# A hybrid encoder's odd layer: tiles placed ahead of the decay sums, low parts of the first group made on chip, state products in two banks

## The chip, the cores and the metric

The kernel runs on one core of one Trainium2 chip. The metric is the device time of one execution in microseconds, the median of several. A core has a TensorE (PE, matmuls), a VectorE (DVE), a ScalarE (ACT), a GpSimd (POOL) and a SyncE (SP, which here only issues DMAs). TensorE writes to PSUM, from which VectorE and ScalarE read.

## The reference

Two layers and a last RMSNorm, on x of 512 positions by 1024, all in fp32. The even layer (latent attention beside a Conformer convolution) is not touched. The odd layer projects the normed x by one matrix and splits the result: a gate z, the convolved x, B and C of a bidirectional Mamba-2 mixer (24 heads in four groups), its raw time steps, and a short gated convolution:

```python
dt_f = jax.nn.softplus(dt_f_raw + dt_bias_f)            # 512 x 24, the same backward
a_f = -jnp.exp(a_log_f)
dA = (dt * a).reshape(b, c, l, g, r)                    # chunks of 128 positions
a_cs = jnp.cumsum(jnp.moveaxis(dA, 2, -1), axis=-1)     # sums of the decays in a chunk
L = jnp.exp(jnp.where(tri, a_cs[..., :, None] - a_cs[..., None, :], -jnp.inf))
...
decay_states = jnp.exp(a_cs[..., -1:] - a_cs)
states = jnp.einsum("bclgn,bcgrl,bclgrp->bcgrpn", Bc, decay_states, X)
```

The state that enters a chunk is the decayed state of the chunk before plus that chunk's product, in both directions.

## The kernel before, in words

A product of fp32 matrices is made of three passes of a reduced type (fp32r): each operand is split into a high part and a low part, and high x high, high x low and low x high are summed. A *channel tile* is 128 output channels of the odd projection by all 512 positions: 24 matmuls of 128x512, 16 with the high part of the weights and 8 with the low part (`mm_cm`, L317).

`Weights._prepare` (L79) brings a tile's weights: a load on SP into `w_raw`, a cast on ScalarE to `w_hi` (L91), and the low part `w_lo`. For the even layer and the z tiles that is one subtraction on VectorE or GpSimd (L96). For the other odd tiles (`BY_DMA`) ScalarE writes the negated high part (L93 in the listing, `w_lo` holding the negated copy), and a DMA issued by GpSimd adds `w_raw` to it on its way (L94). The buffers form small rings; a tile's load waits until the raw buffer's earlier user has been read, and its cast until TensorE has read the earlier high part.

The odd layer's tiles come in a fixed list: z, then C0, B0, x0, x1, x2, zc3, C1, ... `fill(n)` (L791) emits the next n tiles, and turns of earlier tiles behind them. A z tile also yields the raw steps `dtr`. The decay steps follow: softplus by an exponential (L804, ScalarE) and a chain of small VectorE operations on 128x192 (L805 to L817), which ends in `d1`, the product of step and decay. For each direction, `d1` is transposed on TensorE (L823, through the helper at L273), summed along the positions by four scans (L829), written to memory (`acs`, L830), and its sums `cs` are transposed back (L832); from these follow `nacs`, the chunk totals (L836) and the factors `dec`, `ea` and `eA`.

`ssd_states` (L882) makes, for a group, six state products (three chunks, two directions) of 128x384 in PSUM (L891); for the first chunk ScalarE copies the product, for the later ones GpSimd scales the state before (L896) and VectorE adds the product to it (L897). `bank` names the PSUM banks: acc has 3, cv 1, sb 2 and tp 2. Transposes of later work also use them. After the states come the transposes of the group before's normed output (`xs`, scaled at L984).

The order on each engine is set by a scheduler that places the emitted instructions; the code's order and the buffers are what it starts from. In the listings, `kc` holds the identity matrix, `d_4891` (or `d_4834` after) is `d1`.

Of the kernel before, what the change touches and what calls it, by code (L numbers as in the profile page):

```python
# [66 lines left out]
BY_DMA = ("C", "B", "x", "zc", "h", "gc", "gb", "zd")  # L67
EARLY = ("qkv", "a", "g", "uq", "uv", "uk", "zb", "za")


class Weights:
# [7 lines left out]
    def _prepare(self):  # L79
        nc = self.tc.nc  # L80
        key, ap, kt, n = self.slabs[self.i]
        eng = nc.vector if key in EARLY or key in ("oe", "oo") and self.i % 2 else nc.gpsimd
        self.i += 1
        more = key in BY_DMA and self.i % 3 == 0
        raw = (self.more if more else self.pool).tile([P, D], F32, name="w_raw", tag="w_raw",
                                                      bufs=1 if more else self.raw_bufs)[:, :kt * n]
        nc.sync.dma_start(raw, ap)
        more = key in BY_DMA and self.i % 4 == 0
        hi, lo = ((self.more if more else self.pool).tile([P, D], F32R, name=nm, tag=nm, bufs=1 if more else self.bufs)
                  [:, :kt * n] for nm in ("w_hi", "w_lo"))  # L90
        nc.scalar.copy(hi, raw)  # L91
        if key in BY_DMA:
            nc.scalar.mul(lo, raw, -1.0)  # L93
            nc.gpsimd.dma_start(lo, raw, accum_op=ALU.add)  # L94
        else:
            eng.tensor_tensor(lo, raw, hi.bitcast(F32), op=ALU.subtract)  # L96
        v = lambda t: t.rearrange("p (k n) -> p k n", k=kt)
        self.ready.append((key, v(hi), v(lo)))
# [5 lines left out]
    def next(self, key):  # L104
        self.fetch(self.ahead + (3 if key in BY_DMA else 1))
        k, hi, lo = self.ready.pop(0)
        assert k == key, (k, key)
        return hi, lo
# [69 lines left out]
def trunk(ctx, tc, A, out, dbg=None):  # L178
    nc = tc.nc
# [28 lines left out]
    def bank(tag):  # L208
        return ps.tile([P, S], F32, name=tag, tag=tag, bufs=banks[tag])
# [59 lines left out]
    def transposed(blocks, tag="tp", rows=P):  # L269

        tp = bank(tag)
        for j, b in enumerate(blocks):
            T.transpose(tp[:rows, j * P:(j + 1) * P], b, ident)  # L273
        return tp[:rows, :]
# [42 lines left out]
    def mm_cm(key, xT, kk=KT):  # L317

        wh, wl = W.next(key)
        a = bank("acc")  # L320
        xh, xl = xT
        seq = [p for k in range(kk) for p in ((wh[:, k], xh[k]), (wh[:, k], xl[k]))]
        seq += [(wl[:, k], xh[k]) for k in range(kk)]
        for n, (l, r) in enumerate(seq):
            T.matmul(a, l, r, start=n == 0, stop=n == 3 * kk - 1)  # L325
        return a
# [105 lines left out]
    for nm, o, w in (("q_norm", 0, 384), ("kv_norm", 384, 256)):  # L432
# [10 lines left out]
        for k in range(w // P):  # L443
            tp = transposed([qkv[t][:, o + k * P:o + (k + 1) * P] for t in range(NT)])
# [55 lines left out]
    tp = transposed([kr[:, t] for t in range(NT)], "tp", 96)  # L500
# [99 lines left out]
    for p in range(8):  # L600
# [15 lines left out]
        z = mm_cm("zb", xT)  # L616
# [19 lines left out]
    for h in range(2):  # L636
        for t in range(NT):
            tp = transposed([u[h * 4 + j][:, t * P:(t + 1) * P] for j in range(4)], "tp")
# [58 lines left out]
    def bc(col, n, w):  # L697

        return col.rearrange("p (n o) -> p n o", o=1).broadcast_to([P, n, w])

    def over_t(row, n):

        return row.rearrange("p (o n) -> p o n", o=1).broadcast_to([P, NT, n])
# [3 lines left out]
    def one(shape, name, dt=F32):  # L707
        return pg.tile(shape, dt, name=name)

    def tmp(name, tag, bufs, shape=(P, S), dt=F32):  # L710
        return pg.tile(list(shape), dt, name=name, tag=tag, bufs=bufs)

    def prow(nm):
        return rc[:, RC[nm][0]:RC[nm][0] + RC[nm][1]]
# [76 lines left out]
    def fill(n):  # L791

        for _ in range(n):
            before = list(turns)
            turns.clear()
            channel_tile(*next(todo))
            for t in before:
                t()

    fill(2)  # L800

    d1, d2, d3, dt = (one([P, NT, NH], n) for n in ("d1", "d2", "d3", "dt"))
    V.scalar_tensor_tensor(d1, dtr, -1.0, dtr, op0=ALU.mult, op1=ALU.min)
# [11 lines left out]
    aexp = one([P, NH], "aexp")  # L815
    SC.activation(aexp, prow("a_log"), AF.Exp)
    V.scalar_tensor_tensor(d1, dt, -1.0, over_t(aexp, NH), op0=ALU.mult, op1=ALU.mult)  # L817

    nacs = one([P, NT, NH], "nacs")
    acs = dr.tile([2, SH, S], F32, name="acs")  # L820
    back = bank("tp")
    for d in range(2):
        tp = transposed([d1[:, t, d * SH:(d + 1) * SH] for t in range(NT)], "tp", SH)  # L823
        cs = tmp("cs", "c5", 4)[:SH]
        for c in range(NT):
            o, i, z = cs[:, c * P:(c + 1) * P], tp[:, c * P:(c + 1) * P], ident[:SH]
            if d:
                o, i = o[:, ::-1], i[:, ::-1]
            V.tensor_tensor_scan(o, i, z, 0.0, op0=ALU.add, op1=ALU.bypass)  # L829
        nc.sync.dma_start(acs[d], cs)  # L830
        for c in range(NT):
            T.transpose(back[:, c * NH + d * SH:c * NH + (d + 1) * SH], cs[:, c * P:(c + 1) * P], ident[:SH, :SH])  # L832
    V.tensor_scalar(nacs, back[:, :NT * NH].rearrange("p (t h) -> p t h", t=NT), -1.0, None, op0=ALU.mult)
# [18 lines left out]
    def gw(name, bufs):  # L852
        return tmp(name, name, bufs, (P, GW))
# [4 lines left out]
    def heads(g):  # L858
        return [slice(d * SH + g * HPG, d * SH + (g + 1) * HPG) for d in range(2)]

    def ssd_products(g):

        CT, BT = inp[g]["C"], inp[g]["B"]
        cb = bank("tp")
        for c in range(NT):
            cc = slice(c * P, (c + 1) * P)
            T.matmul(cb[:, cc], BT[:, cc], CT[:, cc], start=c == 0, stop=c == 3, skip_group_check=True)
        cbm = [tmp("cbm", "cbm", 4) for _ in range(2)]
        for d in range(2):
            V.tensor_tensor(c4(cbm[d]), c4(cb), masks[d], op=ALU.mult)  # L870
        return cbm, [weighted(g, 0, d) for d in range(2)]

    def chunk(n, d):
        return NT - 1 - n if d else n

    def weighted(g, n, d):

        w, c = gw("gt", 5), chunk(n, d)
        V.tensor_tensor(h3(w), h3(inp[g]["x"][:, c]), bc(dec[:, c, heads(g)[d]], HPG, HD), op=ALU.mult)
        return w  # L880

    def ssd_states(g, first):  # L882

        Bt = inp[g]["Bt"]
        St = [[None] * NT for _ in range(2)]
        for n in range(NT - 1):
            for d in range(2):
                c, nxt = chunk(n, d), chunk(n + 1, d)
                w = weighted(g, n, d) if n else first[d]
                sp = bank("tp")  # L890
                T.matmul(sp[:, :GW], Bt[:, c * P:(c + 1) * P], w, start=True, stop=True)  # L891
                st = St[d][nxt] = gw("St", 12)
                if n == 0:
                    SC.copy(st, sp[:, :GW])
                else:
                    G.tensor_tensor(h3(st), h3(St[d][c]), bc(eA[:, c, heads(g)[d]], HPG, HD), op=ALU.mult)  # L896
                    V.tensor_tensor(st, sp[:, :GW], st, op=ALU.add)  # L897
        return St
# [122 lines left out]
        op[1].append(lo)  # L1021


    fill(5)
    cbm, first = ssd_products(0)
    St = ssd_states(0, first)
    for g in range(GRP):
# [131 lines left out]
```

## Time and profile before

| what | value |
|---|---|
| median of 3 runs | 958.86 us (955.78 to 959.15) |
| the profiled execution, as timed | 958.48 us |
| its span in the trace | 956.7 us |
| TensorE busy | 920.2 us, 96% |
| VectorE / ScalarE / GpSimd busy | 696.0 / 507.7 / 310.1 us |

The span is the time from the first to the last instruction in the trace; what lies around it is 1.78 us. The layers follow one another: the odd layer's first z tiles run from about 505 us, C0 from 518, the four groups of the mixer from about 560 to 860. A wait of an engine stands in brackets behind the instruction that ended it, with the instruction that released it.

### The profile page before, as it was taken

How to read it: one execution, taken by the hardware profiler on the slowest of the kernel's cores; microseconds unless marked ns; L12 is line 12 of the kernel's file. 1: busy time of each engine (PE TensorE's matmuls, PEld its weight loads, DVE VectorE, ACT ScalarE, POOL GpSimd, SP SyncE). 2: the span in 40 equal slices, each digit the busy share in tenths (PEclk: the TensorE clock that was granted, in tenths of full speed). 3: DMA queues.
4: the chain of work that ended last, by engine and by line, in shares of the span. 5: the costliest groups of instructions: out<-in, count | busy, mean ns of one | idle time of the engine just before them, and what ended most of it. 6: DMA issues, size and time to landing. Idle time of an engine off the chain costs nothing.

```text
span 956.7 us, 12593 instructions
## 1 busy us (share of the span) xinstructions
PE 920.2 (96%) x4528; PEld 741.1 (77%) x4528; DVE 696.0 (73%) x1292; ACT 507.7 (53%) x964; POOL 310.1 (32%) x269
## 2 busy tenths in 40 slices
PE   7899998999999999999999899999999999999996
PEld 7888686776877677888889578878786886888885
DVE  4699888999988999893163779777866886466315
ACT  6645454544554444373135487777667757444322
POOL 0142716347073443283222121121212222234222
PEclk9999999999999999999999899999999999999998
DMA  8303302212122215423347679868676776732222
GB/s 317 106 28 112 57 22 95 60 51 86 45 70 83 66 56 97 132 92 111 96 161 201 158 211 220 195 157 214 163 196 159 215 170 161 196 113 74 88 81 88
DMA packets 48373, 119.57 MB, mean 125 GB/s; under 512 B 12808, under 2 KB 14472, under 8 KB 48312
## 3 DMA queue, kind: packets, MB, share of 16 engines
q1 hardware_dynamic: 35304, 82.61, 26.7%
q0 software_dynamic: 6480, 23.60, 13.7%
q10 hardware_dynamic: 6528, 12.58, 4.4%
q8 instruction: 35, 0.57, 0.2%
q14 instruction: 26, 0.21, 0.1%
HBM read 90.85 MB, written 4.33 MB: 99 GB/s over the span
## 4 chain that ended last, share of the span: by engine, by line
PE 79%; DVE 13%; DMA 3%; ACT 3%; issue 1%; POOL 0%; SPq 0%; DVEq 0%; ACTq 0%; POOLq 0%
PE acc L325 39%; PE acc L352 10%; PE tp L352 5%; PE sb L352 5%; PE sb L536 5%; PE tp L273 5%; PE acc L573 3%; PE cv L352 3%; PE cv L945 2%; PE tp L961 1%; DMA sums_d<-sums 1%; ACT w_hi L91 1%; PE sb L273 1%; DVE w_lo L96 1%; DMA w_raw<-in_w_cm_o 1%
## 5 line engine op out<-in xcount | busy, mean ns | idle before, releaser
L325 PE MATMUL acc<-xT_hi,w_hi 128*128 128x512 f32 x616 | 249.2, 406 | 2.7 <-ACT xT_hi L413 2.7
L325 PE MATMUL acc<-xT_lo,w_hi 128*128 128x512 f32 x616 | 246.7, 401 | 0.1
L91 ACT CAST w_hi<-w_raw 128x1024 fp32r<-128x1024 f32 (+7 forms) x139 | 134.8, 971 | 200.8 <-PE acc L325 85.6
L325 PE MATMUL acc<-xT_hi,w_lo 128*128 128x512 f32 x616 | 155.1, 391 | 0.0
L96 DVE TENSOR_TENSOR w_lo<-w_raw,w_hi 128x1024 fp32r<-128x1024 f32 (+6 forms) x74 | 83.0, 1121 | 88.2 <-ACT w_hi L91 77.6
L325 PEld LDWEIGHTS acc<-xT_hi,w_hi 128*128 128x128 f32 x616 | 116.9, 190 | 27.3 <-ACT xT_hi L413 2.9
L488 DVE SCALAR_TENSOR_TENSOR cv<-u,pc,cv 128x497 f32<-128x497 f32 (+10 forms) x176 | 130.2, 740 | 10.1 <-ACT cv L477 7.7
L325 PEld LDWEIGHTS acc<-xT_lo,w_hi 128*128 128x128 f32 x616 | 116.8, 190 | 24.5 <-POOL xT_lo L414 0.8
L325 PEld LDWEIGHTS acc<-xT_hi,w_lo 128*128 128x128 f32 x616 | 115.4, 188 | 24.1
L94 POOL DMA_DIRECT2D w_lo<-w_raw x45 | 39.2, 871 | 180.5 <-ACT w_lo L93 128.2
L96 POOL TENSOR_TENSOR w_lo<-w_raw,w_hi 128x1024 fp32r<-128x1024 f32 (+1 forms) x20 | 47.7, 2387 | 112.0 <-ACT w_hi L91 104.2
L486 POOL TENSOR_TENSOR side<-side 128x510 f32<-128x510 f32 (+3 forms) x56 | 78.6, 1403 | 4.7
L491 POOL TENSOR_TENSOR u<-cs,side 128x512 f32<-128x512 f32 x8 | 11.0, 1375 | 157.1 <-issue 149.9
L540 ACT ACTIVATE p<-sb,mx 128x512 f32<-128x512 f32 x64 | 43.4, 683 | 20.8 <-DVE mx L538 20.5
L485 POOL TENSOR_SCALAR side<-u,pc 128x510 f32<-128x510 f32 (+3 forms) x56 | 50.2, 897 | 4.7
L93 ACT ACTIVATE w_lo<-w_raw 128x1024 fp32r<-128x1024 f32 x45 | 47.5, 1056 | 2.2 <-PE acc L325 2.2
L928 DVE SCALAR_TENSOR_TENSOR e<-e,nacs 128x128 f32<-128x128 f32 x96 | 30.1, 347 | 22.6 <-ACT e L927 22.5
L538 DVE TENSOR_REDUCE mx<-sb 128x1 f32<-128x512 f32 x64 | 41.7, 685 | 3.2 <-PE sb L536 2.6
L923 DVE SCALAR_TENSOR_TENSOR f<-cbm,dt,f 128x128 f32<-128x128 f32 x96 | 39.2, 444 | 5.6 <-ACT f L922 5.6
L273 PEld LDWEIGHTS tp<-kc,p 128*128 128x128 f32 x256 | 28.9, 140 | 16.1 <-ACT pt L563 10.7
L728 DVE SCALAR_TENSOR_TENSOR c<-acc,pc,c 128x510 f32<-128x510 f32 (+1 forms) x48 | 35.8, 745 | 6.3 <-ACT c L726 5.7
L536 PE MATMUL sb<-k_t,qk_hi 128*128 128x512 f32 (+1 forms) x128 | 39.5, 403 | 0.4 <-DVE k_t L264 0.4
(325 smaller groups left out, 1836.8 us busy)
## 6 DMA issues: line engine op xcount, KB each, us to landing
w_raw<-in_w_cm_o SPq DMA_DIRECT2D x45, 512.0 KB, 4.8
w_lo<-w_raw POOLq DMA_DIRECT2D x45, 512.0 KB, 5.9
w_raw<-in_w_cm_e SPq DMA_DIRECT2D x32, 512.0 KB, 3.5
e<-acs ACTq DMA_DIRECT2D x24, 512.0 KB, 6.0
w_raw<-in_w_out_e SPq DMA_DIRECT2D x16, 512.0 KB, 3.5
w_raw<-in_w_out_o SPq DMA_DIRECT2D x16, 512.0 KB, 3.3
xt<-in_xT SPq DMA_DIRECT2D x8, 256.0 KB, 5.1
x_t<-in_x SPq DMA_DIRECT2D x4, 512.0 KB, 6.3
```

Source lines behind the costliest of these rows:

```text
L91: nc.scalar.copy(hi, raw)
L93: nc.scalar.mul(lo, raw, -1.0)
L96: eng.tensor_tensor(lo, raw, hi.bitcast(F32), op=ALU.subtract)
L273: T.transpose(tp[:rows, j * P:(j + 1) * P], b, ident)
L325: T.matmul(a, l, r, start=n == 0, stop=n == 3 * kk - 1)
L352: T.matmul(accs[t][:, :n], l, r, start=k1 == 0 and c == 0, stop=end and c == len(seq) - 1)
L485: G.tensor_scalar(t[:, o], ut[:, i], wt(j), 0.0, op0=ALU.mult, op1=ALU.add)
L486: G.tensor_tensor(side[:, o], side[:, o], t[:, o], op=ALU.add)
L488: V.scalar_tensor_tensor(c[:, o], ut[:, i], wt(j), c[:, o], op0=ALU.mult, op1=ALU.add)
L536: T.matmul(s, l[:, qs], r, start=n == 0, stop=n == 2)
L538: V.tensor_reduce(mx, s, axis=AX.X, op=ALU.max, negate=True)
L540: SC.activation(p, s, AF.Exp, bias=mx, accum_out=sums[:, q:q + 1])
```

## The change

Three things. The first group's five tiles behind z (C0, B0, x0, x1, x2) get their low parts by a subtraction on chip: B0 and x1 on VectorE, C0, x0 and x2 on GpSimd. Second, one tile is emitted ahead of the decay steps instead of two, one behind them and one between the scans and the transposes back, which now come for both directions together and go to the `cv` bank; four instead of five tiles follow; `acs` is written from ScalarE's queue. Third, the state products of the second direction go to `sb` instead of `tp`.

```diff
--- before.py
+++ after.py
@@ -79,7 +79,9 @@
     def _prepare(self):
         nc = self.tc.nc
         key, ap, kt, n = self.slabs[self.i]
-        eng = nc.vector if key in EARLY or key in ("oe", "oo") and self.i % 2 else nc.gpsimd
+        z = [k for k, _, _, _ in self.slabs].index("z")
+        add = key in BY_DMA and self.i >= z + 9
+        eng = nc.vector if key in EARLY or key in ("oe", "oo", "B", "x") and self.i % 2 else nc.gpsimd
         self.i += 1
         more = key in BY_DMA and self.i % 3 == 0
         raw = (self.more if more else self.pool).tile([P, D], F32, name="w_raw", tag="w_raw",
@@ -89,7 +91,7 @@
         hi, lo = ((self.more if more else self.pool).tile([P, D], F32R, name=nm, tag=nm, bufs=1 if more else self.bufs)
                   [:, :kt * n] for nm in ("w_hi", "w_lo"))
         nc.scalar.copy(hi, raw)
-        if key in BY_DMA:
+        if add:
             nc.scalar.mul(lo, raw, -1.0)
             nc.gpsimd.dma_start(lo, raw, accum_op=ALU.add)
         else:
@@ -797,7 +799,7 @@
             for t in before:
                 t()
 
-    fill(2)
+    fill(1)
 
     d1, d2, d3, dt = (one([P, NT, NH], n) for n in ("d1", "d2", "d3", "dt"))
     V.scalar_tensor_tensor(d1, dtr, -1.0, dtr, op0=ALU.mult, op1=ALU.min)
@@ -815,10 +817,11 @@
     aexp = one([P, NH], "aexp")
     SC.activation(aexp, prow("a_log"), AF.Exp)
     V.scalar_tensor_tensor(d1, dt, -1.0, over_t(aexp, NH), op0=ALU.mult, op1=ALU.mult)
+    fill(1)
 
     nacs = one([P, NT, NH], "nacs")
     acs = dr.tile([2, SH, S], F32, name="acs")
-    back = bank("tp")
+    back, css = bank("cv"), []
     for d in range(2):
         tp = transposed([d1[:, t, d * SH:(d + 1) * SH] for t in range(NT)], "tp", SH)
         cs = tmp("cs", "c5", 4)[:SH]
@@ -827,7 +830,10 @@
             if d:
                 o, i = o[:, ::-1], i[:, ::-1]
             V.tensor_tensor_scan(o, i, z, 0.0, op0=ALU.add, op1=ALU.bypass)
-        nc.sync.dma_start(acs[d], cs)
+        nc.scalar.dma_start(acs[d], cs)
+        css.append(cs)
+    fill(1)
+    for d, cs in enumerate(css):
         for c in range(NT):
             T.transpose(back[:, c * NH + d * SH:c * NH + (d + 1) * SH], cs[:, c * P:(c + 1) * P], ident[:SH, :SH])
     V.tensor_scalar(nacs, back[:, :NT * NH].rearrange("p (t h) -> p t h", t=NT), -1.0, None, op0=ALU.mult)
@@ -887,7 +893,7 @@
             for d in range(2):
                 c, nxt = chunk(n, d), chunk(n + 1, d)
                 w = weighted(g, n, d) if n else first[d]
-                sp = bank("tp")
+                sp = bank(("tp", "sb")[d])
                 T.matmul(sp[:, :GW], Bt[:, c * P:(c + 1) * P], w, start=True, stop=True)
                 st = St[d][nxt] = gw("St", 12)
                 if n == 0:
@@ -1021,7 +1027,7 @@
         op[1].append(lo)
 
 
-    fill(5)
+    fill(4)
     cbm, first = ssd_products(0)
     St = ssd_states(0, first)
     for g in range(GRP):
```

On TensorE around tile x0, before, from the end of tile B0 on: `d_4891` is transposed for one direction, `cs` is transposed back between matmuls, and then the second direction follows.

```order
L325 MATMUL acc<-xT_hi,w_lo 128x512 x8
L325 MATMUL acc<-xT_hi,w_hi 128x512
L273 MATMUL tp<-kc,d_4891 24x128 x4
L325 MATMUL acc<-xT_lo,w_hi 128x512
L325 MATMUL acc<-xT_hi,w_hi 128x512
L325 MATMUL acc<-xT_lo,w_hi 128x512
L832 MATMUL tp<-kc,cs 128x24
L325 MATMUL acc<-xT_hi,w_hi 128x512
```

The same place after the change:

```order
L327 MATMUL acc<-xT_hi,w_lo 128x512 x8
L327 MATMUL acc<-xT_hi,w_hi 128x512
L327 MATMUL acc<-xT_lo,w_hi 128x512
L327 MATMUL acc<-xT_hi,w_hi 128x512
L327 MATMUL acc<-xT_lo,w_hi 128x512
L327 MATMUL acc<-xT_hi,w_hi 128x512
L275 MATMUL tp<-kc,d_4834 24x128 x8
L327 MATMUL acc<-xT_lo,w_hi 128x512
L838 MATMUL cv<-kc,cs 128x24
L327 MATMUL acc<-xT_hi,w_hi 128x512
```

Four matmuls of x0 have moved ahead of the transposes of `d`, all eight of these stand together, and one matmul instead of three stands between them and the first transpose of `cs`.

On ScalarE, before, from the cast of B0's weights to the exponential of the decay steps (`d_4891<-d_4891`) and the cast of x2's weights behind it; L91 are the casts of B0, x0, x1 and x2, L93 the negations, L359 the gates of z:

```order
L91 CAST w_hi<-w_raw 128x1024
L93 ACTIVATE w_lo<-w_raw 128x1024
L91 CAST w_hi<-w_raw 128x1024
L359 ACTIVATE zg<-sb 128x384
L93 ACTIVATE w_lo<-w_raw 128x1024
L359 ACTIVATE zg<-sb 128x384
L359 ACTIVATE zg<-tp 128x384
L91 CAST w_hi<-w_raw 128x1024
L359 ACTIVATE zg<-tp 128x384
L93 ACTIVATE w_lo<-w_raw 128x1024
L804 ACTIVATE d_4891<-d_4891 128x192
L91 CAST w_hi<-w_raw 128x1024
```

and after the change, where the first row holds the casts of C0, B0 and x0:

```order
L93 CAST w_hi<-w_raw 128x1024 x3
L361 ACTIVATE zg<-sb 128x384 x2
L361 ACTIVATE zg<-tp 128x384
L93 CAST w_hi<-w_raw 128x1024
L361 ACTIVATE zg<-tp 128x384
L806 ACTIVATE d_4834<-d_4834 128x192
L93 CAST w_hi<-w_raw 128x1024
```

The negations between these casts are gone, and the exponential stands behind the same four gates and the cast of x1's weights.

On TensorE in the third group's states, before, from the second pair of products (`tp<-gt,Bt`) to the transposes of `xs`:

```order
L891 MATMUL tp<-gt,Bt 128x384 x2
L325 MATMUL acc<-xT_lo,w_hi 128x512
L325 MATMUL acc<-xT_hi,w_hi 128x512
L325 MATMUL acc<-xT_lo,w_hi 128x512
L891 MATMUL tp<-gt,Bt 128x384
L325 MATMUL acc<-xT_hi,w_hi 128x512
L325 MATMUL acc<-xT_lo,w_hi 128x512
L325 MATMUL acc<-xT_hi,w_hi 128x512
L325 MATMUL acc<-xT_lo,w_hi 128x512
L325 MATMUL acc<-xT_hi,w_hi 128x512
L891 MATMUL tp<-gt,Bt 128x384
L273 MATMUL tp<-kc,xs 128x128 x4
```

and after, from the first product on:

```order
L897 MATMUL tp<-gt,Bt 128x384
L897 MATMUL sb<-gt,Bt 128x384
L897 MATMUL tp<-gt,Bt 128x384
L897 MATMUL sb<-gt,Bt 128x384
L897 MATMUL tp<-gt,Bt 128x384
L897 MATMUL sb<-gt,Bt 128x384
L275 MATMUL tp<-kc,xs 128x128 x2
L327 MATMUL acc<-xT_hi,w_hi 128x512
```

The six products stand together, directions alternating between the two banks, and the transposes of `xs` come at once behind them; before, matmuls of a channel tile stood between.

## Rows read from the trace of the kernel before

**Rows 1.** The page: busy time, share and instructions of TensorE over the span, and the granted clock of TensorE in 40 slices of the span, in tenths.

```profile
PE 920.2 (96%) x4528; PEld 741.1 (77%) x4528; DVE 696.0 (73%) x1292; ACT 507.7 (53%) x964; POOL 310.1 (32%) x269
...
PEclk9999999999999999999999899999999999999998
```

**Rows 2.** The list of TensorE's waits over the span: what waited, for whom, the us in total, how often, and the longest.

```profile
PE tp L273 <- DVE d L817: 4.3, 1, 4.3
PE tp L891 <- DVE St L897: 3.9, 6, 1.2
```

**Rows 3.** The timeline of TensorE from the end of tile C0 to the first matmul of tile x1. Columns: start, us from the first instruction's start to the last one's end, engine, line, operation, out<-in, count, and in brackets the idle time before it with its releaser.

```profile
521.79 1.98 PE L325 MATMUL acc<-xT_hi,w_lo 128*128 128x512 f32 x8
...
529.05 0.39 PE L325 MATMUL acc<-xT_hi,w_hi 128*128 128x512 f32 x1
533.73 0.60 PE L273 MATMUL tp<-kc,d 128*24 128x128 f32 x4 [4.30 <-DVE d L817]
...
542.86 0.24 PE L832 MATMUL tp<-kc,cs 24*128 24x24 f32 x1
...
543.45 0.24 PE L832 MATMUL tp<-kc,cs 24*128 24x24 f32 x1
...
546.03 0.39 PE L325 MATMUL acc<-xT_hi,w_hi 128*128 128x512 f32 x1
```

**Rows 4.** The timeline of TensorE at 42.50 (columns as in rows 3), and two stretches of the span with their length, the busy time of each engine (and its instructions), TensorE's granted clock as a share of full speed, DMA share and GB/s.

```profile
42.50 1.28 PE L325 MATMUL acc<-xT_hi,w_hi 128*128 128x512 f32 x3 [2.70 <-ACT xT_hi L413]
...
42.50:47.00 4.50, 4.40 (x12) 3.03 (x13) 4.50 (x7) 3.47 (x11) 4.04 (x3) 0.62 0.20 74
533.70:542.00 8.30, 8.27 (x26) 5.01 (x26) 5.39 (x13) 1.17 (x2) 0.86 (x1) 0.59 0.89 209
```

**Rows 5.** The timeline of ScalarE from the cast of C0's weights to the exponential of the decay steps.

```profile
508.74 1.05 ACT L91 CAST w_hi<-w_raw 128x1024 fp32r<-128x1024 f32 x1 [1.05 <-PE tp L352]
...
522.12 1.05 ACT L91 CAST w_hi<-w_raw 128x1024 fp32r<-128x1024 f32 x1 [3.86 <-DMA w_raw<-in_w_cm_o]
...
524.41 0.35 ACT L804 ACTIVATE d<-d 128x192 f32<-128x192 f32 x1
```

**Rows 6.** The chain of waits in order of time, 505 to 535: two loads of weights, start and time from the issue to the landing.

```profile
509.85 3.29 DMA w_raw<-in_w_cm_o
...
516.11 5.92 DMA w_raw<-in_w_cm_o
```

**Rows 7.** The timeline of VectorE along the decay steps, from the negated minimum (L803) to the scans.

```profile
519.09 0.36 DVE L803 SCALAR_TENSOR_TENSOR d<-dtr 128x192 f32<-128x192 f32 x1
...
523.60 0.56 DVE L360 SCALAR_TENSOR_TENSOR zg<-zg,tp 128x384 f32<-128x384 f32 x1 [3.86 <-ACT zg L359]
524.79 0.26 DVE L805 TENSOR_SCALAR d<-d 128x192 f32<-128x192 f32 x1 [0.64 <-ACT d L804]
525.09 1.35 DVE L806 RECIPROCAL d<-d 128x192 f32<-128x192 f32 x1
...
527.56 1.54 DVE L811 SCALAR_TENSOR_TENSOR d<-d,d 128x192 f32<-128x192 f32 x4
...
533.22 0.36 DVE L817 SCALAR_TENSOR_TENSOR d<-dt,aexp 128x192 f32<-128x192 f32 x1
533.50 0.68 DVE L730 SCALAR_TENSOR_TENSOR CT<-c5t,CT 128x512 f32<-128x512 f32 x1
...
534.36 1.35 DVE L829 TENSOR_TENSOR_SCAN cs<-tp,kc 24x128 f32<-24x128 f32 x4
```

**Rows 8.** The page's groups of the subtractions that make low parts, on VectorE and on GpSimd: busy time, mean ns of one | idle before, releaser.

```profile
L96 DVE TENSOR_TENSOR w_lo<-w_raw,w_hi 128x1024 fp32r<-128x1024 f32 (+6 forms) x74 | 83.0, 1121 | 88.2 <-ACT w_hi L91 77.6
...
L96 POOL TENSOR_TENSOR w_lo<-w_raw,w_hi 128x1024 fp32r<-128x1024 f32 (+1 forms) x20 | 47.7, 2387 | 112.0 <-ACT w_hi L91 104.2
```

**Rows 9.** Two timelines near 408 us, VectorE's first and GpSimd's last line.

```profile
406.86 0.69 DVE L660 SCALAR_TENSOR_TENSOR ln_v<-ln_th,ln_v 128x512 f32<-128x512 f32 x1
...
408.87 0.69 DVE L360 SCALAR_TENSOR_TENSOR oT<-oT,acc 128x512 f32<-128x512 f32 x1
409.58 2.25 DVE L660 SCALAR_TENSOR_TENSOR ln_v<-ln_th,ln_v 128x512 f32<-128x512 f32 x1
...
408.87 2.41 POOL L96 TENSOR_TENSOR w_lo<-w_raw,w_hi 128x1024 fp32r<-128x1024 f32 x1
```

**Rows 10.** The third group's state products and what follows: TensorE's timeline (a product counts as two instructions there), one line of VectorE's, and the stretch as a whole (columns as in rows 4).

```profile
716.02 1.46 PE L891 MATMUL tp<-gt,Bt 128*128 128x384 f32 x4
...
718.40 1.58 PE L891 MATMUL tp<-gt,Bt 128*128 128x384 f32 x4 [0.70 <-ACT St L894]
719.52 0.69 PE L325 MATMUL acc<-xT_lo,w_hi 128*128 128x512 f32 x1
720.05 0.39 PE L325 MATMUL acc<-xT_hi,w_hi 128*128 128x512 f32 x1
...
721.83 0.91 PE L891 MATMUL tp<-gt,Bt 128*128 128x384 f32 x2 [1.15 <-DVE St L897]
...
724.94 0.60 PE L273 MATMUL tp<-kc,xs 128*128 128x128 f32 x4
...
721.69 1.97 DVE L984 TENSOR_SCALAR xs<-xs,rs 128x384 f32<-128x384 f32 x4
...
715.00:726.00 11.00, 8.87 (x37) 5.27 (x36) 10.25 (x31) 7.51 (x20) 4.37 (x5) 1.00 0.28 90
```

## The prediction

> **What bounds the kernel now.** I read the totals first. TensorE is busy for 96% of the 956.7 us, and its granted clock shows one dent besides the edges [rows 1]. So time can come only from stretches where TensorE waits or runs at its lower level. The list of its waits names the two that the change is aimed at [rows 2]: 4.3 us once for the decay steps (`d`, L817), and 3.9 us in six waits for the states' sums (L897).
>
> Then I read the place of the first wait in time [rows 3]. Channel tile x0 starts at 529.05, does one matmul, and TensorE stands 4.30 us until the transposes of `d` at 533.73. The next tile, x1, starts at 546.03, so 12.30 us lie between those transposes and x1. The clock rows say why so long: from 533.70 to 542.00 the granted clock is 0.59, so 8.30 x 0.41 = 3.40 us are lost [rows 4]. The same thing stands once earlier in the trace: after 2.70 us of idleness ending at 42.50, the granted clock is 0.62 over 4.50 us, 1.71 us lost [rows 4]. A mean of about 0.6 is a mix of the two levels, 1.2 and 2.4 GHz. At the full clock the 12.30 us would be 8.90.
>
> Why `d` is late is read from ScalarE and VectorE. The exponential that begins the decay steps (L804) comes at 524.41, behind the cast of x1's weights at 522.12 and the last gate [rows 5]. That cast had waited 3.86 us for its weights: their load could be issued only at 516.11, and took 5.92 [rows 6]. What held it was the raw buffer of C0, which the accumulate DMA still read. From L805 at 524.79 to the end of L817 at 533.58 the chain on VectorE takes 8.79 us [rows 7].
>
> **First part: low parts on chip.** For five tiles the negation (L93) and the accumulate DMA go; C0, x0 and x2 are subtracted on GpSimd, B0 and x1 on VectorE. The nearest durations are 2.39 us on GpSimd and 1.12 on VectorE [rows 8].
> - C0 is cast at 508.74 to 509.79 [rows 5]; its subtraction on GpSimd takes 2.39 and ends at 512.2, and x1's load is issued at 512.3 instead of 516.11. With 3.29 to 5.92 us for a load [rows 6] it lands at 515.6 to 518.2.
> - x1's cast also needs the buffer that the last z tile reads until 518.1, where C0's matmuls begin [rows 3]; it runs about 517.9 to 519.0, then the last gate, then the exponential. Its input on VectorE (L803) was ready at 519.45 already [rows 7], so it ends about 519.9 instead of 524.76.
> - VectorE then does x1's subtraction (1.12, until 520.6) and the last gate's product (0.56, as in the row at 523.60 [rows 7]). The chain starts at 521.1, 3.7 us earlier.
> - Into the chain come L813 (a step that stood ahead of it; 0.30, as L805 takes until the reciprocal begins) and CT's last product (L730, whose row gives 0.68 [rows 7]; with its wait for ScalarE some 0.75). So it takes 8.79 + 0.30 + 0.75 = 9.84 and would end at 531.0, with the transposes at 531.1.
>
> **What stands against it: x2's subtraction on GpSimd.** It waits for x2's cast and for the buffer of C0's low parts, which TensorE reads until 523.8 (the eight matmuls at 521.79, 1.98 us [rows 3]). So it runs about 523.9 to 526.3, in the middle of the chain, whose steps from L811 on read two operands from SBUF. The trace shows what that does [rows 9]: the same VectorE step L660 takes 0.69 alone and 2.25 when it begins at 409.58 beside a GpSimd subtraction of 408.87 to 411.28; it ends just 0.55 behind it. Beside that same subtraction L360, with one operand in PSUM, keeps its 0.69. The first L811 would be due at 524.1, so the chain stops for 2.2 us and ends at 533.2, with the transposes at 533.3. If the chain were only slowed in part, the cost would lie between 0 and 2.4 (a whole subtraction). I take 2.2, since the row shows the step standing until the other's end.
>
> The Trainium skill says this too (SBUF — State Buffer, "SBUF: two separate sides"): VectorE and GpSimd share a pair of ports as an exclusive lock for a whole instruction, and a VectorE operation with two SBUF inputs falls under it. By that rule the chain waits the whole remainder, 2.2 us; had the row shown the two slowing each other instead, half of that would do, and the sum would be about 2 us shorter. The row agrees with the lock.
>
> **Second part: tiles ahead.** Before the transposes of `d`, TensorE now does five matmuls of x0 instead of one, and then both directions' transposes at once. With 24 matmuls in 5.44 us (a pace of 0.227, from the start of C0's eight last at 521.79 and of x0 at 529.05, 32 matmuls in 7.26 [rows 3]) it comes to the transposes at 529.05 + 5 x 0.227 = 530.2. Unblocked, the wait would be 0.9; with the block 3.1, instead of 4.30. Behind the transposes stand the 8.90 us of before less the four matmuls done ahead (0.91), plus 0.2 for the first scan, which now has one matmul ahead of it instead of three: 8.2. The pairs of one transpose of `cs` and one matmul take 0.59 at the full clock [rows 3]; a scan takes 0.34 (1.35 for four [rows 7]), so later scans keep ahead. A wait of 3.1 us lies between the 2.70 and the 4.30 that both ended with a lower clock, so I charge 1.71 + 0.4/1.6 x 1.69 = 2.1. x1 then starts at 533.3 + 8.2 + 2.1 = 543.6 against 546.03: 2.4 us gained. Bounds of this term: 6.7 gained (transposes at 531.1, no loss of clock, x1 at 539.3) and 0.1 lost (the wait as long as before and the full 3.40 of lost clock: 530.2 + 4.3 + 8.2 + 3.4).
>
> The `acs` writes move to ScalarE's queue, where they wait for a direction's scans; behind them stands C1's cast, which waits for x0's matmuls anyway. If that cover is gone, the cast is late by under one scan set, 1.35. SP's loads no longer stand behind these writes; no wait of TensorE in the list is for such a load there, so nothing. The five negations and DMAs saved lie on engines that are not late elsewhere: nothing.
>
> **Third part: state products in two banks.** Each group's six products now run without matmuls between them. In the third group they start at 716.02, wait 0.70 and 1.15 on the way, and the transposes of `xs` follow at 724.94 [rows 10]. At 0.5 us a product (a pair starts 1.00 before the next matmul) and with four buffers they would end about 719.0 to 719.5; but VectorE scales `xs` only from 721.69 [rows 10], first part done at 722.2. So TensorE stands 2.5 us in one piece, where before it stood 1.85 in two with matmuls between. The first two groups have 14 and 12 matmuls behind the products, which cover this; there I estimate 1 us gained in each, from four changes between the two kinds of matmul fewer: one matmul of a tile behind products takes 0.53 (719.52 to 720.05 [rows 10]) instead of 0.227, so 0.3 a change. In the last two the waiting is gathered up, and one of 2.70 was followed by 1.71 us of lost clock [rows 4], while 1.15 here was not (the granted clock stayed at 1.00 [rows 10]). One such loss, plus the matmuls of the last group that no longer fill its wait, takes the 2 us back. I take 0 for this part; bounds 4.6 gained (the 3.9 of L897 and the 0.70 in rows 10) and 5.1 lost (three falls of the clock).
>
> **The sum.** The profiled execution took 958.48 us, 1.78 of it outside the span. 958.48 - 2.4 - 0 = 956.1. It lies 0.4 below the median of 958.86, and the runs of before spread over 3.4, so I do not correct for it.
>
> **Rivals.**
> 1. The subtraction of x2 does not stop the chain (it falls into the reciprocal of 1.35 us, or behind the chain). Then x1 starts at 539.3, 6.7 earlier: 951.8. For it: the times of cast and chain are known to about 1 us only. Against it: the chain is ten microseconds long and x2's weights become due in its middle. 0.20.
> 2. The gathered waits at the transposes of `xs` bring the clock down in three groups, at 1.71 each, with nothing gained at the products: 958.48 - 2.4 + 5.1 = 961.2, slower than before. It decides from a wait of about 2.70 on. For it: my 2.5 us in the third group and the same pattern in the fourth; against it: VectorE sets the pace there, so a part of a slow stretch is hidden. 0.12.
> 3. The change does not remove the wait: x1's weights land late; at the same landing as before, 522.0, the chain starts at 524.8 and, 9.84 long, ends at 534.6 or behind. Then TensorE gains only the four matmuls and loses them to a longer chain: 958.5. For it: one load takes 3.29 and the next 5.92 [rows 6], so their times are not steady; against it: it would have to take almost 10 from its earlier issue, and the accumulate traffic that stood beside it is gone. 0.13.
> The forecast keeps 0.55.
>
> **How the numbers follow.** About 0.5% (4.8 us) is what a measurement of this kernel can tell from no change, so faster means under 954.1 and slower over 963.7. Rival 1 is nearly all faster (0.18), and a sixth to a quarter of the forecast's own range (953 to 959) and its neighbours is too, if the clock holds: together 0.30. Rival 2 reaches over the bound only if its waits come near 4.30 (3.40 each), which is half its chance, and a few hundredths of rival 3 if the chain is blocked as well: 0.08. The rest, 0.62, is no change to be told. The range goes from 950.5 (rival 1 and a microsecond of the states) to 961.2 (rival 2).
>
> **What would show it.** The cast of x1 at about 518 with no wait for its load, and the exponential at about 519.6: the first part. A VectorE step of about 2.5 us at 524, ending 0.3 behind a GpSimd subtraction: the block. A wait of about 3 us at the transposes of `d` and a granted clock near 0.5 behind it: my price; a wait under 1 us and a clock of 1.00 would show rival 1. One wait of 2 to 3 us at the transposes of `xs` in the last two groups in place of those at the products shows the third part. I am wrong if the products' waits disappear without a new one (then 951 to 953), or if the chain starts no earlier.

## The result and the profile after

Over 20 runs each, the changed kernel has a median of 961.95 us and the kernel before 958.14. The ratio is 1.0032 (95% interval 1.0016 to 1.0047): the change makes the kernel slower by a third of a per cent. (One run of 1141.76 us, at a mean granted clock of 0.752, is left out of the ratio; without it the median is 961.81.) The single runs lie from 953.73 to 965.24, two and a half times the width of before (955.78 to 960.44), and on the whole they follow the mean granted clock: 953.73 came with 0.992, 965.24 with 0.983. (That width is not the change's alone: in 34 later runs the kernel before spread from 954.04 to 964.24.) The profiled execution took 964.13 us (span 962.4) at 0.981.

The page, busy TensorE and its clock in 40 slices, and from the list of TensorE's waits the two that answer to [rows 2]:

```profile
PE 927.2 (96%) x4528; PEld 749.0 (78%) x4528; DVE 698.0 (73%) x1294; ACT 503.0 (52%) x959; POOL 313.1 (33%) x267
...
PEclk9999999999999999999999799999999999999998
```

```profile
PE tp L275 <- DVE xs L990: 7.2, 4, 2.6
...
PE tp L275 <- DVE d L819: 2.4, 1, 2.4
```

The wait for `d` has gone from 4.3 to 2.4 us. The states' sums (L897 before, L903 now) are no longer waited for at all; in their place stand 7.2 us in four waits for the scaling of `xs`, none of which the list of before had. TensorE is busy 7.0 us longer for the same work, and the clock rows say why: a matmul takes longer at the lower level. (Some 1.7 us were lost in the even layer, between 151 and 156 us, behind a wait of 1.81 us; the change does not touch that place, so this much of the execution's 964.13 is not its doing.)

The stretches around x0 and around the transposes of `xs` in the second to fourth group (columns as in [rows 4]; the third number from the end is the granted clock):

```profile
530.00:560.00 30.00, 27.58 (x103) 19.79 (x102) 17.74 (x37) 12.82 (x19) 2.75 (x3) 0.77 0.47 116
645.00:660.00 15.00, 13.10 (x57) 10.47 (x56) 8.65 (x28) 6.62 (x11) 4.13 (x5) 0.89 0.74 190
720.00:735.00 15.00, 12.25 (x51) 9.12 (x50) 10.19 (x24) 8.59 (x16) 4.49 (x5) 0.89 0.52 140
798.00:815.00 17.00, 14.44 (x63) 11.31 (x63) 11.49 (x29) 10.79 (x22) 5.52 (x6) 0.90 0.64 160
```

Lost to the clock: 30 x 0.23 = 6.9 us around x0, and 15 x 0.11, 15 x 0.11 and 17 x 0.10, about 1.7 each, in the groups: 11.9 in all. Before, the only loss in the odd layer's tiles was the 3.40 around x0.

The places themselves on TensorE, which answer to [rows 3] and [rows 10]: the transposes of `d` and the start of x1, and the first transposes of `xs` in the three groups.

```profile
529.64 0.39 PE L327 MATMUL acc<-xT_hi,w_hi 128*128 128x512 f32 x1
...
533.35 1.34 PE L275 MATMUL tp<-kc,d 128*24 128x128 f32 x8 [2.42 <-DVE d L819]
...
547.64 0.39 PE L327 MATMUL acc<-xT_hi,w_hi 128*128 128x512 f32 x1
...
648.86 0.41 PE L275 MATMUL tp<-kc,xs 128*128 128x128 f32 x2 [1.90 <-DVE xs L990]
...
724.58 0.30 PE L275 MATMUL tp<-kc,xs 128*128 128x128 f32 x1 [2.24 <-DVE xs L990]
...
802.63 0.41 PE L275 MATMUL tp<-kc,xs 128*128 128x128 f32 x2 [2.56 <-DVE xs L990]
```

x0 starts at 529.64, 0.6 later than before (this execution is that much later already where the odd layer begins), and x1 at 547.64: 18.00 us against 16.98. In the groups TensorE stands 1.90, 2.24 and 2.56 us for the scaled `xs`.

### The profile page after: what moved, and what is told of

It is laid out like the page before. It is cut to its first block, busy times and chain, and to the rows that moved or that the text cites. A ratio compares the mean times of both kernels' runs of the same rounds, so it can differ in the third digit from the quotient of the medians.

```text
span 962.4 us, 12588 instructions
## 1 busy us (share of the span) xinstructions
PE 927.2 (96%) x4528; PEld 749.0 (78%) x4528; DVE 698.0 (73%) x1294; ACT 503.0 (52%) x959; POOL 313.1 (33%) x267
## 3 DMA queue, kind: packets, MB, share of 16 engines
q0 software_dynamic: 5760, 20.97, 11.9%
## 4 chain that ended last, share of the span: by engine, by line
PE 77%; DVE 13%; DMA 4%; ACT 4%; issue 1%; POOL 0%; SPq 0%; DVEq 0%; ACTq 0%; POOLq 0%
PE acc L327 38%; PE acc L354 8%; PE tp L354 5%; PE sb L354 5%; PE tp L275 5%; PE sb L538 5%; PE acc L575 3%; PE cv L354 3%; PE cv L951 2%; DVE cv L490 2%; PE tp L967 1%; DMA w_raw<-in_w_cm_e 1%; DVE w_lo L98 1%; DMA e<-acs 1%; ACT w_hi L93 1%
## 5 line engine op out<-in xcount | busy, mean ns | idle before, releaser
L93 ACT CAST w_hi<-w_raw 128x1024 fp32r<-128x1024 f32 (+7 forms) x139 | 134.5, 970 | 205.3 <-PE acc L327 86.3
L327 PE MATMUL acc<-xT_hi,w_lo 128*128 128x512 f32 x616 | 157.4, 395 | 0.0
L98 DVE TENSOR_TENSOR w_lo<-w_raw,w_hi 128x1024 fp32r<-128x1024 f32 (+6 forms) x76 | 85.7, 1128 | 95.5 <-ACT w_hi L93 84.9
L98 POOL TENSOR_TENSOR w_lo<-w_raw,w_hi 128x1024 fp32r<-128x1024 f32 (+1 forms) x23 | 55.0, 2393 | 121.2 <-ACT w_hi L93 107.2
L96 POOL DMA_DIRECT2D w_lo<-w_raw x40 | 35.0, 874 | 175.1 <-ACT w_lo L95 129.4
L95 ACT ACTIVATE w_lo<-w_raw 128x1024 fp32r<-128x1024 f32 x40 | 42.3, 1056 | 2.2 <-PE acc L327 2.2
```

## The experiments

The theory after this: two separate losses. GpSimd's subtraction of x2 stops VectorE's chain, so the wait for `d` stays long enough to bring the clock down; and the products in two banks gather the waiting of three groups into one wait each, with the same effect. The rivals: the loss is all made around x0 (by the longer chain, or by the run of small transposes), or the two banks cost by themselves. The first four kernels take the change apart, the next four mend one loss or both, the last two profile the changed kernel again. A profile shows one execution, so its time is given where it lies far from the kernel's median.

**The third part undone, the first two kept.**

```diff
-                sp = bank(("tp", "sb")[d])
+                sp = bank("tp")
```

> The changed kernel with its third part undone: all state products in the two tp banks again, parts one and two kept. Theory (the gathered waits at the transposes of xs bring the clock down in three groups): the granted clock stays at 1.00 in 640 to 820, the time falls by about 4.5 us against the changed kernel's 962, to some 957.5; the stretch behind the transposes of d stays as in the changed kernel (a wait of about 2.4 us, 6 to 7 us of lost clock). Rival (the loss is made around x0 alone, and the third part is neutral because its saved waits pay for the clock): 961 to 962.

Measured: 955.3 us, ratio to before 0.9965 (0.9945 to 0.9985): faster than expected. Its profiled execution shows this at the transposes of `d`, on TensorE's timeline, and in the same stretches of the span:

```profile
527.10 0.39 PE L327 MATMUL acc<-xT_hi,w_hi 128*128 128x512 f32 x1
...
530.86 1.03 PE L275 MATMUL tp<-kc,d 128*24 128x128 f32 x8 [2.47 <-DVE d L819]
...
539.49 0.40 PE L327 MATMUL acc<-xT_hi,w_hi 128*128 128x512 f32 x1
```

```profile
530.00:560.00 30.00, 29.14 (x141) 23.00 (x142) 21.73 (x43) 18.28 (x33) 3.63 (x4) 1.00 0.75 183
640.00:655.00 15.00, 14.53 (x69) 11.44 (x68) 8.95 (x24) 9.24 (x17) 3.19 (x4) 1.00 0.91 210
715.00:730.00 15.00, 14.73 (x69) 11.49 (x68) 9.30 (x20) 8.82 (x15) 3.46 (x5) 1.00 0.68 167
790.00:807.00 17.00, 16.56 (x79) 12.98 (x80) 9.41 (x23) 11.89 (x24) 3.69 (x5) 1.00 0.59 162
```

The groups keep the full clock, as the theory has it. Around x0 the theory's last clause fell: the wait is 2.47 us, longer than in the changed kernel, and the clock stayed at 1.00; x0 took 12.39 us. This execution (951.85) is the fastest of the twelve; the median (955.3) lies 3.4 above it, and single runs reach 958.5. So other executions probably do lose something (none of them was profiled), but this one shows that such a wait need not.

**The third part alone, on the kernel before.**

```diff
-                sp = bank("tp")
+                sp = bank(("tp", "sb")[d])
```

> The kernel before with the third part alone (the second direction's products in sb). Theory: waits of 1.9 to 2.6 us at the transposes of xs in three groups, each followed by 3 to 4 us at half the clock, 1.7 us lost each; slower than before by 3 to 5 us, 961 to 963. Rival: no more than 1 us from before, 957 to 959.

Measured: 962.36 us, ratio 1.0049 (1.0028 to 1.0070), as the theory expected. The waits and the groups' stretches:

```profile
PE tp L273 <- DVE xs L984: 7.1, 4, 2.6
```

```profile
645.00:660.00 15.00, 13.13 (x64) 10.51 (x63) 9.35 (x28) 7.85 (x13) 3.48 (x4) 1.00 0.84 209
720.00:735.00 15.00, 12.30 (x53) 9.43 (x53) 9.86 (x23) 8.19 (x14) 4.59 (x6) 0.89 0.56 149
798.00:815.00 17.00, 14.43 (x65) 11.63 (x64) 10.08 (x27) 10.81 (x22) 3.98 (x5) 0.90 0.67 164
```

The same 7 us of waits; but the wait of the second group (1.87 us) left the clock at 1.00, and only the other two brought it down. Around x0, where this kernel is the same as before, TensorE waited 5.11 us for `d` and the clock lost 5.1 us (0.83 over 530 to 560) instead of 3.4; so a part of this execution's time is not the third part's.

**The first part alone, on the kernel before** (the `add` line, the choice of engine and `if add:`; everything else as before).

```diff
+        z = [k for k, _, _, _ in self.slabs].index("z")
+        add = key in BY_DMA and self.i >= z + 9
-        eng = nc.vector if key in EARLY or key in ("oe", "oo") and self.i % 2 else nc.gpsimd
+        eng = nc.vector if key in EARLY or key in ("oe", "oo", "B", "x") and self.i % 2 else nc.gpsimd
...
-        if key in BY_DMA:
+        if add:
```

> The kernel before with the first part alone (low parts of the first five tiles on chip). Theory (x2's subtraction on GpSimd stops the chain of VectorE for 2.2 us): the exponential comes some 4 us earlier, the transposes of d only 0.5 to 1.5 us earlier; a wait of about 3 us stays and the clock still falls; 956.5 to 958. Rival (the block is harmless, since the chain starts so much earlier): the wait under 1 us, no fall of the clock, 951 to 953.

Measured: 956.06 us, ratio 0.9976 (0.9956 to 0.9996): slightly faster, 0.4 below the theory's range. The transposes of `d`:

```profile
533.13 0.60 PE L275 MATMUL tp<-kc,d 128*24 128x128 f32 x4 [2.76 <-DVE d L819]
```

A wait of 2.76 us, and the clock fell: read by the microsecond, 6.8 us were lost, as many as in the changed kernel, though the second part, with its eight transposes together, is not in this kernel. x0 took 17.70 us in this execution, the slowest of the twelve (961.79). Six of the runs lie from 952.20 to 954.17 and six from 957.94 to 961.79, as they would if the clock fell in half of them; only this one was profiled.

**The second part alone** (the changed kernel with parts one and three undone: one tile ahead of each step, both directions together, `back` in cv, `acs` on ScalarE's queue).

```diff
-    fill(2)
+    fill(1)
...
+    fill(1)
...
-    back = bank("tp")
+    back, css = bank("cv"), []
...
-        nc.sync.dma_start(acs[d], cs)
+        nc.scalar.dma_start(acs[d], cs)
+        css.append(cs)
+    fill(1)
+    for d, cs in enumerate(css):
...
-    fill(5)
+    fill(4)
```

> The kernel before with the second part alone (one tile ahead of each step, both directions together, back in cv, acs from ScalarE's queue). Theory: the wait for d falls from 4.3 to about 3.5 by the four matmuls done ahead, but the clock falls as before, and the eight pairs of one small transpose and one matmul keep it down longer (6 to 7 us lost instead of 3.4); 959 to 961. Rival (the low clock lasts by the length of the wait): 957 to 958.

Measured: 961.08 us, ratio 1.0032 (1.0013 to 1.0051): the size came out as the theory said, but the profile does not show its reason. The profiled execution is by far the fastest of the twelve (954.23; the others lie from 960.59 to 964.52), so what most of them lose stays open. TensorE's wait and, on ScalarE, the cast of x2's weights ahead of C0's convolution:

```profile
530.55 1.87 PE L273 MATMUL tp<-kc,d 128*24 128x128 f32 x8 [4.87 <-DVE d L817]
```

```profile
524.86 1.05 ACT L91 CAST w_hi<-w_raw 128x1024 fp32r<-128x1024 f32 x1 [4.46 <-DMA w_raw<-in_w_cm_o]
525.81 0.77 ACT L726 ACTIVATE CT<-acc,pc 128x512 f32<-128x512 f32 x1
```

The wait grew to 4.87 instead of falling to 3.5. The chain on VectorE has C0's convolution (L728) among its steps, whose input from ScalarE (L726, at 525.81) stands behind a cast that waited 4.46 us for x2's load; in the changed kernel, where no accumulate DMA stands before it, that cast begins at 522.58. And the transposes of `d` came to stand among B0's last matmuls, so no matmuls of x0 lay ahead of them. Read by the microsecond, the clock was at its lower level for some 6.8 us here, with the eight pairs of a small transpose and a matmul as in the changed kernel, where it was 13.6 (6.8 lost at half the clock); so in this execution the pairs did not keep it down. Alone, part two costs 2.9 us (961.08 against 958.14); on top of part one it moved the median by 0.8 (956.06 to 955.3), which the intervals do not tell from nothing.

**x2's low part by DMA again, all else as changed.**

```diff
-        add = key in BY_DMA and self.i >= z + 9
+        add = key in BY_DMA and self.i >= z + 8
```

> The changed kernel, but x2's low part is made by the negation and the accumulate DMA again, so that no GpSimd subtraction lies beside the chain of VectorE. Theory (that subtraction stops the chain for 2.2 us): no step of the chain over 0.4 us, the transposes of d 2 us earlier, a wait under 0.6 us there and the clock at 1.00 from 530 to 560; the third part's loss stays; about 957 to 958. Rival (the clock around x0 falls for the many small transposes, whatever the wait): the wait is short too, but the granted clock falls behind 534 as in the changed kernel; 960 to 962.

Measured: 955.62 us, ratio to before 0.9966 (0.9947 to 0.9986), 6.3 below the changed kernel's median and 1.4 better than expected. First VectorE in the changed kernel, then GpSimd there, then VectorE and TensorE here:

```profile
521.74 0.25 DVE L807 TENSOR_SCALAR d<-d 128x192 f32<-128x192 f32 x1
...
524.54 3.31 DVE L813 SCALAR_TENSOR_TENSOR d<-d,d 128x192 f32<-128x192 f32 x3
```

```profile
524.44 2.41 POOL L98 TENSOR_TENSOR w_lo<-w_raw,w_hi 128x1024 fp32r<-128x1024 f32 x1 [6.16 <-PE acc L327]
```

```profile
521.24 0.25 DVE L807 TENSOR_SCALAR d<-d 128x192 f32<-128x192 f32 x1
...
524.03 1.15 DVE L813 SCALAR_TENSOR_TENSOR d<-d,d 128x192 f32<-128x192 f32 x3
```

```profile
530.68 1.03 PE L275 MATMUL tp<-kc,d 128*24 128x128 f32 x8 [0.62 <-DVE d L819]
...
539.31 0.40 PE L327 MATMUL acc<-xT_hi,w_hi 128*128 128x512 f32 x1
```

The three first steps of L813 take 3.31 us with GpSimd's subtraction of 2.41 beside them, and 1.15 without: 2.16 us, the block as predicted. Without it the wait for `d` is 0.62 instead of 2.42, and x0 takes 539.31 - 528.77 = 10.54 us. What is left of the third part:

```profile
530.00:560.00 30.00, 29.38 (x143) 23.14 (x143) 21.73 (x43) 18.31 (x33) 3.45 (x4) 1.00 0.82 202
639.00:654.00 15.00, 13.29 (x58) 10.88 (x59) 7.74 (x22) 7.66 (x11) 2.10 (x2) 0.89 0.76 210
714.00:729.00 15.00, 12.69 (x54) 10.28 (x55) 9.44 (x21) 7.16 (x14) 3.56 (x4) 0.89 0.55 143
793.00:810.00 17.00, 15.87 (x79) 12.98 (x80) 8.60 (x23) 12.21 (x24) 3.31 (x4) 1.00 0.65 158
```

```profile
794.07 0.41 PE L275 MATMUL tp<-kc,xs 128*128 128x128 f32 x2 [2.58 <-DVE xs L990]
```

Around x0 the clock is 1.00, though the many small transposes are all still there; it is 1.00 there too in the profiles of the other two kernels with x2 by DMA. So the rival, that the transposes bring it down whatever the wait, has three executions against it. Two groups lose 1.65 us each; in the last, a wait of 2.58 us left the clock alone.

**The same, and the third part undone.** Both one-line edits above together.

> As the run before this, and the third part undone too. Theory: the clock is 1.00 from 530 to 820 in every run, about 951.5 to 952.5, and less spread than the kernel without the third part (951.9 to 958.5), since no wait over 1.3 us is left in the odd layer. Rival (the spread has other causes): a median near 955 and the same spread.

Measured: 951.39 us, ratio 0.9931 (0.9908 to 0.9955), runs from 950.48 to 955.11. As the theory expected, the granted clock of its profile is 1.00 in every stretch from 530 to 820, the wait for `d` is 0.3 us, x0 takes 10.23. That it is so in every run is not shown: the run of 955.11 had a mean of 0.990, against 0.995 to 0.998 in the others.

**The tile behind the state products.** The changed kernel, with one line moved.

```diff
             ssd_norm(g)
-            fill(1)
             St = ssd_states(g + 1, first)
+            fill(1)
             ssd_turn(g)
```

> The changed kernel with one line moved: the tile that was emitted ahead of the later groups' state products comes behind them, so that 15 to 19 matmuls stand between the products and the transposes of xs. Theory (the third part costs by the waits gathered at the transposes of xs): these waits fall from 1.9 to 2.6 us to under 0.7 each and the clock is 1.00 from 640 to 820; 957 to 958.5, what is left being the stretch around x0. Rival (the products in two banks cost by themselves, or VectorE sets the pace): the waits come back at another place and the time stays at 961 to 962.

Measured: 954.34 us, ratio 0.9958 (0.9935 to 0.9981), 7.6 below the changed kernel and better than expected. The transposes of `xs` in the three groups:

```profile
648.13 0.41 PE L275 MATMUL tp<-kc,xs 128*128 128x128 f32 x2 [1.36 <-DVE xs L990]
...
725.94 0.68 PE L275 MATMUL tp<-kc,xs 128*128 128x128 f32 x4 [0.57 <-DVE xs L990]
...
800.38 0.68 PE L275 MATMUL tp<-kc,xs 128*128 128x128 f32 x4 [0.59 <-DVE xs L990]
```

The waits are 1.36, 0.57 and 0.59 (the first is over the 0.7 that was expected), and the granted clock is 1.00 in 640 to 660, 720 to 740 and 790 to 820. (In 660 to 720 it is 0.97, behind a wait of 2.87 us for a convolution's last step at 688.83, away from the states.) So the two banks do not cost by themselves. x0 is as slow here as in the changed kernel (18.02 us), since x2's subtraction is still on GpSimd; the execution (960.29) is the slowest of the twelve. The moved line was not tried on the kernel before, so what it gains without the third part is open.

**Both.** x2 by DMA, and the tile behind the state products.

> The changed kernel with both: x2's low part by DMA, and the tile behind the state products. Theory: both losses go, 950.5 to 952, at or a little below the kernel without the third part and with x2 by DMA. Rival (what is gained at the products comes back as a wait on VectorE later): 953 or more.

Measured: 949.25 us, ratio 0.9913 (0.9884 to 0.9943), runs from 947.9 to 954.24: faster than both kernels, 1.3 better than expected, 9.2 us below the kernel before, measured beside it (958.4), and 12.7 below the changed one. The stretches around x0 and the groups:

```profile
530.00:560.00 30.00, 30.00 (x141) 23.53 (x141) 21.73 (x42) 19.24 (x38) 2.84 (x4) 1.00 0.82 211
637.00:652.00 15.00, 13.57 (x66) 10.87 (x65) 9.04 (x25) 9.18 (x16) 2.96 (x3) 1.00 0.76 212
713.00:728.00 15.00, 14.44 (x72) 11.63 (x71) 9.35 (x27) 9.61 (x17) 1.74 (x2) 1.00 0.67 158
788.00:805.00 17.00, 16.42 (x84) 13.28 (x83) 9.29 (x29) 13.02 (x24) 1.74 (x2) 1.00 0.68 168
```

All four at the full clock. (In 660 to 720 it is 0.97 here too, behind a wait of 1.73 us for a convolution's last step at 678.17.) It lies 2.1 below the kernel with x2 by DMA and one bank pair (951.39): with its wait covered, the third part looks like a gain, though the intervals of the two ratios overlap.

**The changed kernel, profiled twice more.**

> The changed kernel, unchanged, looked at once more. Theory (waits of 1.9 to 2.6 us bring the clock down in some executions and not in others): the same four waits within 0.3 us, but at least one of the four stretches (x0, and three groups) with another granted clock than in the first look, and the time moved by what that stretch loses. Rival (the fall is set by the code and the wait): the same clock in the same stretches, 962 to 965.

> As the run before this, a third look at the same code: theory and rival as there.

Measured: 960.98 and 957.31 us. The waits are the same: 2.47 and 2.43 for `d`, 1.91 and 1.91, 2.25 and 2.23, 2.56 and 2.56 for `xs`. The clock is not:

```profile
530.00:560.00 30.00, 28.62 (x120) 21.77 (x121) 20.17 (x41) 16.13 (x27) 3.62 (x4) 0.89 0.64 156
640.00:655.00 15.00, 13.03 (x62) 10.17 (x61) 8.97 (x29) 7.45 (x14) 4.17 (x5) 1.00 0.74 205
```

```profile
530.00:560.00 30.00, 28.80 (x130) 22.61 (x131) 20.50 (x41) 17.07 (x28) 3.62 (x4) 0.94 0.69 167
640.00:655.00 15.00, 13.12 (x57) 10.92 (x58) 7.71 (x24) 7.47 (x11) 2.14 (x3) 0.89 0.75 210
```

Around x0 the clock was 0.77, 0.89 and 0.94 in the three executions (6.9, 3.3 and 1.8 us lost, or 6.8, 3.4 and 1.7 read by the microsecond; x0 took 18.00, 15.32 and 13.93 us), and in the second group 0.89, 1.00 and 0.89. The rival, a fixed loss for a fixed wait, is out.

Nor does the fall always stand next to the wait. In the third execution the clock stayed at full speed behind the transposes of `d` and fell at about 536.8, in the last of the pairs, where a matmul's time goes from 0.49 to 0.78:

```profile
531.20 1.03 PE L275 MATMUL tp<-kc,d 128*24 128x128 f32 x8 [2.43 <-DVE d L819]
...
536.13 0.49 PE L327 MATMUL acc<-xT_hi,w_hi 128*128 128x512 f32 x1
...
536.72 0.78 PE L327 MATMUL acc<-xT_lo,w_hi 128*128 128x512 f32 x1
```

In the second it fell at the wait, rose, and fell again at about 538.2. With a short wait the same pairs kept 1.00, but no run has the long wait without them, so whether around x0 it is the wait alone, or the wait and the pairs together, is open.

## Why the prediction was wrong

The measured 961.95 lies 0.75 above the range, and the change is slower where a small gain was forecast. Point by point:

- *The first part* was right. x1's cast ran at 519.02 to 520.06 without a wait for its load, the exponential at 520.34, the chain from 521.74 (forecast 521.1, in an execution 0.5 to 0.6 later throughout).
- *The block by x2's subtraction* was right: 2.16 us measured, 2.2 forecast. The exclusive lock that the Trainium skill describes (SBUF — State Buffer, "SBUF: two separate sides") is borne out: the three steps, 0.38 each when undisturbed, end 1.00 us behind GpSimd's subtraction (524.54 + 3.31 against 524.44 + 2.41), so next to nothing of them was done beside it.
- *The wait for* `d` was 2.42 instead of 3.1, since the chain was half a microsecond shorter (521.74 to 533.21, 11.5 instead of 12.0).
- *The clock behind it* was charged at 2.1 us, by interpolating between two waits. It lost 6.9, 3.3 and 1.8 us in three executions of the same code, and 0 in one of the kernel without the third part. As a rule the charge was wrong: the loss does not follow from the wait. The wait at 42.50 that it was in part read from shows this best, since no edit touches that code: it is there in all twelve traces (2.70 or 2.71 us, once 3.21), and behind it 1.7 us were lost in seven, 3.4 in three and nothing in two. Parts one and two together came out at 955.3, a gain of 2.8 against the forecast 2.4; that the two agree is luck, a median over executions that lose nothing there and executions that lose much. (At the full clock the stretch from the transposes to x1 took 8.63 us, 530.86 to 539.49 without the third part, where 8.2 was forecast.)
- *The third part* is the step that failed: "I take 0 for this part". It costs 4.2 us alone (962.36 against 958.14) and 6.7 on top of the other two (961.95 against 955.3). I had the mechanism as rival 2, and the wait of the third group nearly to size (2.24 for 2.5), but two suppositions were wrong. That the second group's 12 matmuls cover its wait: they end at 646.96, and the transposes of `xs` come at 648.86, because there too VectorE scales `xs` last. And that of three gathered waits one would cost the clock: in the first profiled execution all three did, and in each of the other two at least two of the three. Of the 1 us that was to be gained in the second group 0.34 is left: from the first product to the transposes of `xs`, with 12 matmuls between in both, it takes 8.71 us (640.15 to 648.86) against 9.05 (638.37 to 647.42), since the wait has eaten the rest.
- *The chances.* Rival 2 had 0.12 and its time, 961.2, was 0.8 from the result; its mechanism holds, the closeness is partly luck, since its price per fall and the number of falls vary from execution to execution. The result also lies between 954.1 and 963.7, where the prediction put a chance of 0.62, but not by the way it gave. The wait of 1.15 us that had kept the clock and the one of 2.70 that had not left everything between open; 1.9 to 2.6 us at three places was to be taken as more likely than not to bring a fall at least once or twice.

What stays open: why the same wait brings the clock down in one execution and not in the next, why the low level lasted 13.6 us behind a wait of 2.42 us and 6.8 behind 4.30 (twice the 6.8 and 3.4 lost), and why part two alone is slower. The runs show that it differs at equal code, not by what. The Trainium skill (TensorE: Matmul & The Clock Gate, "Part 1: The HAM clock gate") says that the monitor behind the gate runs free of the kernel, so that one kernel meets it differently from run to run. The three executions agree with that; no run here shows the monitor itself.

## What to carry to other kernels

When instructions are gathered into a run, ask which wait they were filling: the time that vanishes between them comes back in one piece at the next thing that a slower engine has to deliver, and on TensorE one piece of 2 us can cost the clock where the two of 0.70 and 1.15 [rows 10] did not. Keep a tile's worth of matmuls for that place (one moved line was worth 7.6 us here). Before work is moved to GpSimd, look at what VectorE does beside it: here steps with two operands in SBUF stood still until the GpSimd instruction had ended, so a low part made by DMA was cheaper than a subtraction of 2.41 us on GpSimd (955.62 against 961.95).

## What the runs showed of the hardware

- VectorE steps with both operands in SBUF stood for as long as GpSimd's subtraction ran: 3.31 against 1.15 us for three of them.
- Equal waits of TensorE had different sequels. Of `d`: 2.42 us (granted clock 0.77 from 530 to 560), 2.47 (0.89), 2.43 (0.94), 2.47 (1.00). Of `xs` in the second group: 1.90 (0.89), 1.91 (1.00), 1.87 (1.00); in the fourth: 2.56 (0.90), 2.58 (1.00). At the transposes of `xs`, waits of 1.36 us and less kept 1.00 in both kernels that had them. The wait of 2.70 us near 42 us was followed by a clock of 0.93 over 36 to 60 us (before), 0.86 (third part alone) and 1.00 (second part alone).
- Between 505 and 945 us of the twelve traces each stretch at the lower level cost 1.7, 3.4, 5.1 or 6.8 us, read by the microsecond; no other loss occurs, so a charge between two of them, such as 2.1, can be right only as a mean.
- Run times spread from 953.7 to 965.2 for the changed kernel and from 950.5 to 955.1 for the one without long waits in the odd layer. These are 19 and six runs, and the kernel before spread over 4.7 us in one series and 10.2 in another, so the narrower spread is a hint and no more.
